# Modulation work moved to earlier FFNs, and four more FFN tiles by seven products, in a two-layer hybrid trunk

## The chip, the cores and the metric

The kernel runs on one core of a Trainium2 chip, in one launch. The metric is the device time of one execution in microseconds (us); 0.2% of it is 5.6 us.

## What is computed

Two layers of a trunk run over 640 tokens of width 1024: 128 of a prompt and 512 of a sample. Each layer has a SwiGLU FFN, a token mixing (state-space scan, long convolution, retention and attention side by side) and a second FFN. Shift, scale and gate of each of these three parts come from a product of the condition with a modulation matrix of 1024 x 9216 per layer.

```python
def trunk_layer(x, cond, lp, ssd_s0, ret_s0, ctx_kv):
    mod = (jax.nn.silu(cond) @ lp['w_mod'] + lp['b_mod'])[:, None, :]
    sh1, sc1, g1, sh2, sc2, g2, sh3, sc3, g3 = jnp.split(mod, N_MOD, axis=-1)
    nw = lp['norm_w']
    x = x + 0.5 * g1 * swiglu(modulate(rmsnorm(x, nw[0]), sh1, sc1), lp['ffn_w_in'][0], lp['ffn_w_out'][0])
    y, s_ssd, s_ret, k, v = token_mixing(modulate(rmsnorm(x, nw[1]), sh2, sc2), lp, ssd_s0, ret_s0, ctx_kv)
    x = x + g2 * y
    x = x + 0.5 * g3 * swiglu(modulate(rmsnorm(x, nw[2]), sh3, sc3), lp['ffn_w_in'][1], lp['ffn_w_out'][1])
```

`swiglu(h)` is `(silu(h @ w_gate) * (h @ w_up)) @ w_out` with an inner width of 2816, that is 22 tiles of 128.

## The kernel before

**Layout.** Activations are kept transposed: 8 tiles of 128 channels by 640 tokens, in two groups g of 320 columns. Every product of float32 values is made of three fp32r matmuls (`mm3`, L88: high by high, high by low, low by high). A weight tile is loaded as `raw` (512 KB), ScalarE casts it to `hi` (L76), and VectorE subtracts to get `lo` (`wsplit`, `tt`, L61); activations are split in the same way (`hh`, `hl`; in the FFN `gh`, `gl`). There are three buffers each of `raw`, `hi` and `lo`, and three PSUM buffers `mm`.

**The FFNs.** There are four: the first (layer 0, before the mixing) is `ffn`, all of its 22 inner tiles direct. The second (layer 0, after the mixing), the third (layer 1, before) and the fourth (layer 1, after) are `ffn7`. In `ffn7` the first `ndir` tiles are direct: a `direct` tile is a gate unit and an up unit for each group, 4 units of 24 matmuls, 96 in all. The other tiles are `quad` tiles: gate and up weights by the two token groups are taken as a product of 2 x 2 blocks, done with seven products instead of eight, 84 matmuls. For this VectorE makes sums of weights (`sa`, `sb`) and `sums(j)` makes sums of the normed tiles (`nv`) and splits them into factors (`th`, `tl`). `NDIR` gives the direct tiles of the second, third and fourth FFN: 2, 12, 2. The inner tiles come in chunks of 5, 5, 5, 4 and 3 (`FFN_CHUNKS`); after each of the first four, `down` multiplies the chunk by the output weights (8 tiles m by 2 groups) and VectorE accumulates into the residual `x` (L70).

**The modulations.** Apart from a few blocks at the start, which TensorE multiplies, VectorE makes all modulations (`modulation`, `modpiece`, L271): a step is a multiply-reduce of a 128x1024 weight tile `wm` against the silu of one of the two conditions (`condb`), output `wmj` being junk, with a row that reads the accumulator. A tile is two steps; a modulation (li, idx) is 8 tiles, 16 steps; `wm` has two buffers (`MBUF`). `todo` lists which modulations are made in which FFN. The FFN's code draws the steps: a rate is added to a credit after each half tile of a direct tile (`rates[0]`), after each m of a `down` (`rates[1]`) and after each quad (`rates[2]`), and a step is issued for each whole credit. What is left is issued before the last chunk.

```python
            def some(rate):
                credit[0] += rate
                while credit[0] >= 1.0:
                    next(mods, None)
                    credit[0] -= 1.0
```

**What sets the order.** The order on each engine is fixed at compile time: a list scheduler takes instructions by priority, largely the program's order, and fills in what is ready. `PIN` (`keep_in_program_order`) pins each modulation step to its place in the program. Each engine and each DMA queue (all loads are issued by SyncE) then runs its own instructions in that order.

Of the kernel before, what the change touches and what calls it, by code (L numbers as in the profile page):

```python
# [53 lines left out]
class Trunk:  # L54
# [486 lines left out]
    def ffn7(self, li, w, todo, ndir, rates, after_group):  # L541
        I, n = self.I, 2 * w
        pool = lambda name: self.tc.tile_pool(name=name, bufs=2, side="right", reuse_waits="tile")
        with pool("ws") as sp, pool("ffn") as mp, pool("mods") as modp, self.tmp():
            mods = self.modulation(todo, modp, bufs=MBUF, pin=PIN) if todo else iter(())
            self.G = []
            credit = [0.0]
# [8 lines that stand above are left out]
            def finish(q):  # L556
                for _ in q:
                    pass

            def down(ff, nk):  # L560

                G, self.G = self.G[:nk], self.G[nk:]
                for m in range(8):
                    hi, lo = self.wload(I["ffnoutA"][li, w, m, :, ff * 128 : (ff + nk) * 128], nk * 128)
                    for g in range(2):
                        ps = self.mmp.tile([128, 512], F32, tag="mm", name="mm")[:, :320]
                        self.mm3(ps, [(hi[:, k * 128 : (k + 1) * 128], lo[:, k * 128 : (k + 1) * 128]) + G[k][g]
                                      for k in range(nk)])
                        self.accumulate(li, n, m, g, ps)
                    some(rates[1])  # L570

            def direct(f):

                ws = [self.wload(I["ffnin"][li, w, 2 * f + i], 1024) for i in range(2)]
                sg = mp.tile([128, 640], F32, tag="sg", name="sg", bufs=2)
                gh = self.ring("gh", 640, F32R)
                gl = self.ring("gl", 640, F32R)
                for g in range(2):
                    c = slice(320 * g, 320 * g + 320)
                    self.act(sg[:, c], self.unit(ws[0], g, shifts=False), AF.Silu)  # L580
                    self.tt(sg[:, c], self.unit(ws[1], g, shifts=False), sg[:, c], MUL)
                    self.split(gh[:, c], gl[:, c], sg[:, c])
                    some(rates[0])
                self.G.append([(gh[:, 320 * g : 320 * g + 320], gl[:, 320 * g : 320 * g + 320]) for g in range(2)])

            ends = [sum(FFN_CHUNKS[: i + 1]) for i in range(len(FFN_CHUNKS))]
            for f in range(ndir):
                direct(f)
                if f < 2:
                    self.sums(f)  # L590
                if f + 1 in ends:
                    nk = FFN_CHUNKS[ends.index(f + 1)]
                    down(f + 1 - nk, nk)
            for j in range(2):
                self.split(self.hw[0][1][:, 2 * j : 2 * j + 2, 0:320], self.hw[1][1][:, 2 * j : 2 * j + 2, 0:320], self.V[0][j])
            prev = None
            for f in range(ndir, 22):
                q = self.quad(li, w, f, sp, mp, f == 21)
                next(q)
                if prev is not None:  # L600
                    next(prev)
                next(q)
                if prev is not None:
                    finish(prev)
                    if f in ends:
                        ci = ends.index(f)
                        down(f - FFN_CHUNKS[ci], FFN_CHUNKS[ci])
                prev = q
                some(rates[2])
            finish(prev)  # L610
            for _ in mods:
                pass
            nk = FFN_CHUNKS[-1]
            ws = [self.wload(I["ffnoutB"][li, w, b], 1024) for b in range(3)]
            G = self.G
            for g in range(2):
                for m in range(8):
                    if g and m == NPOS:
                        next(done, None)
                    ps = self.mmp.tile([128, 512], F32, tag="mm", name="mm")[:, :320]  # L620
                    parts = []
                    for k in range(nk):
                        b, j = divmod(m * nk + k, 8)
                        parts.append((ws[b][0][:, j * 128 : (j + 1) * 128],
                                      ws[b][1][:, j * 128 : (j + 1) * 128]) + G[k][g])
                    self.mm3(ps, parts)
                    self.accumulate(li, n, m, g, ps)
                    if li + 1 < NL or w == 0:
                        self.square(m, g)
                if g:  # L630
                    next(done, None)
                done = after_group(g)
                next(done, None)
            next(done, None)
# [777 lines left out]
    def run(self):  # L1412
        self.setup()
        with self.tc.tile_pool(name="start", bufs=2, side="right", reuse_waits="tile") as p, self.tmp():
            nc = self.nc
            cb = self.condb_start(p)
            self.xload(self.I["xT"])
            norms = [self.norm(0, 0, g, nc.vector, True) for g in range(2)]
            scale = self.modulation([(0, 1)], p, tiles=range(4, 8), bufs=SMB, cb=cb)
            shift = self.modulation([(0, 0)], p, tiles=range(2 * SPE, 8), bufs=SMB, cb=cb)  # L1420
            for j in range(2 + SPE):
                self.modulation_start(0, 1 if j < 2 else 0, p, range(j % 2, j % 2 + 1) if j < 4 else range(j - 2, j - 1))
                for gen in (scale, scale) if j < 2 else (shift,):
                    next(gen, None)
                for g in range(2):
                    if j == SORD[g] or j == SORD[2 + g]:
                        next(norms[g], None)
            for _ in shift:
                pass
            self.shifts(0, 0)  # L1430
            ahead = [self.wload(self.I["ffnin"][0, 0, i], 1024) for i in range(2)]
            for n in norms:
                next(n, None)
        kern = self.filters(range(NL))
        todo = [[(0, i) for i in range(2, 9)], [(1, 0), (1, 1)],
                [(1, i) for i in range(2, 8)], [(1, 8)]]
        for li in range(NL):
            def n1(g):
                if g == 0:
                    self.shifts(li, 1)  # L1440
                yield from self.norm(li, 1, g)
                self.xspill(li, g)

            def n2(g):
                yield from self.norm7(li, 2, g)

            def n3(g):
                if li + 1 < NL:
                    yield from self.norm7(li + 1, 0, g)
                else:  # L1450
                    self.store(g)
                    yield

            if li == 0:
                self.ffn(li, 0, todo[0], RATES[0], n1, ahead)
            else:
                self.ffn7(li, 0, todo[2], NDIR[1], RATES[2], n1)
                self.fac.close()
            for m in range(8):
                for g in range(2):  # L1460
                    self.tap(f"x1_{li}_{m}_{g}", self.x[m][g])
            self.mix(li, kern, n2)
            for m in range(8):
                for g in range(2):
                    self.tap(f"x2_{li}_{m}_{g}", self.x[m][g])
            self.ffn7(li, 1, todo[2 * li + 1], NDIR[2 * li], RATES[2 * li + 1], n3)
        self.fac.close()
# [7 lines left out]
RLAG = 1  # L1475
SLAG = 1
SB = 2
NDIR = 2, 12, 2
CB = 3
CGACT = True  # L1480
MBUF = 2
NPOS = 8
RATES = 2.0, (1.5, 1.0, 0.5), (2.2, 1.0, 1.0), (2.0, 1.0, 3.0)
PIN = True
WB = 3
EACT = 1
# [164 lines left out]
```

## Time and profile before

| | before |
|---|---|
| median of 3 runs | 2776.7 us (2774.94 to 2779.11) |
| the profiled execution | 2773.57 us |
| its span in the profile | 2771.8 us |
| granted TensorE clock, mean | 0.988 |
| TensorE busy | 96% |
| VectorE busy | 71% |
| ScalarE busy | 37% |

The span is what lies between the first and the last instruction of the profiled execution. Matmuls are pipelined: one is recorded as some 0.31 us while the next begins about 0.15 us after it, so that a count of matmul records in a stretch tells more than busy time. "mm" and "mb" are PSUM tiles, the second of a quad's first product.

### The profile page before, as it was taken

To read this page: it belongs to the slowest core of one execution; us is meant where nothing else is said; L and a number is where in the kernel's file an instruction comes from. 1 tells how busy PE (TensorE), PEld (TensorE's weight loads), DVE (VectorE), ACT (ScalarE), POOL (GpSimd) and SP (SyncE) were. 2 spreads that over 40 slices of the span, in tenths; PEclk is the share of its full clock that TensorE was granted. 3 is DMA by queue.
4 is the path that set the end of the run, shared out by engine and by line. 5 is a ranking of instruction groups with operands and counts; after the bars stand their busy time and mean duration, and the time that the engine had idled before them with its cause. 6 is when DMAs were issued, how large, how long until landed. Compare 5 with 4: busy or idle time off the path is not lost.

```text
span 2771.8 us, 45385 instructions
## 1 busy us (share of the span) xinstructions
PE 2671.7 (96%) x17870; PEld 2575.6 (93%) x17870; DVE 1959.7 (71%) x4050; ACT 1030.2 (37%) x2042; POOL 114.0 (4%) x191
## 2 busy tenths in 40 slices
PE   5999999999999989999999999998999998999999
PEld 3889999989999979999988999998999997999999
DVE  5886666665685687776667777787658578876666
ACT  3222222242455353433353223334335535343342
POOL 0000000020010020000020000002001002000000
PEclk9999999999999999999999999999999999999999
DMA  7435444431221323333213443334212132322222
GB/s 247 145 125 197 142 135 148 137 103 66 81 78 42 108 69 107 105 111 121 84 61 118 158 149 129 117 130 148 85 57 96 36 106 68 107 79 82 85 69 91
DMA packets 118389, 299.64 MB, mean 108 GB/s; under 512 B 19747, under 2 KB 42483, under 8 KB 117664
## 3 DMA queue, kind: packets, MB, share of 16 engines
q1 hardware_dynamic: 118176, 296.74, 32.6%
q8 instruction: 141, 2.31, 0.3%
q14 instruction: 72, 0.59, 0.1%
HBM read 282.49 MB, written 14.20 MB: 107 GB/s over the span
## 4 chain that ended last, share of the span: by engine, by line
PE 89%; DVE 5%; issue 2%; POOL 1%; ACT 1%; DMA 1%; SPq 0%; POOLq 0%; DVEq 0%; ACTq 0%
PE mm L88 68%; PE mx L88 10%; PE mc L88 6%; PE mb L88 3%; PE mx L93 2%; DVE lo L61 1%; POOL nsum L287 1%; DVE x L70 1%; DVE wmj L271 1%; ACT hi L76 0%; POOL nrs L120 0%; DVE hl L61 0%; DVE tl L61 0%; DVE nv L61 0%; DVE gl L61 0%
## 5 line engine op out<-in xcount | busy, mean ns | idle before, releaser
L88 PE MATMUL mm<-hh,lo 128*128 128x320 f32 (+2 forms) x2936 | 922.8, 315 | 13.0 <-DVE lo L61 13.0
L88 PE MATMUL mm<-hh,hi 128*128 128x320 f32 (+2 forms) x2936 | 927.6, 317 | 6.8 <-ACT hh L76 4.1
L88 PE MATMUL mm<-hl,hi 128*128 128x320 f32 (+2 forms) x2936 | 924.3, 315 | 2.5 <-DVE hl L61 2.1
L76 ACT CAST hi<-raw 128x1024 fp32r<-128x1024 f32 (+3 forms) x390 | 338.5, 868 | 779.0 <-PE mm L88 704.4
L88 PEld LDWEIGHTS mm<-hh,lo 128*128 128x128 f32 (+1 forms) x2936 | 558.8, 190 | 20.3 <-DVE lo L61 14.1
L88 PEld LDWEIGHTS mm<-hh,hi 128*128 128x128 f32 (+1 forms) x2936 | 557.1, 190 | 15.0 <-ACT hh L76 5.7
L88 PEld LDWEIGHTS mm<-hl,hi 128*128 128x128 f32 (+1 forms) x2936 | 556.9, 190 | 12.8 <-issue 5.1
L61 DVE TENSOR_TENSOR lo<-raw,hi 128x1024 fp32r<-128x1024 f32 (+3 forms) x390 | 387.6, 994 | 175.0 <-ACT hi L76 172.9
L88 PE MATMUL mm<-gh,hi 128*128 128x320 f32 x1408 | 438.4, 312 | 5.5 <-DVE x L70 5.5
L88 PE MATMUL mm<-gl,hi 128*128 128x320 f32 x1408 | 436.3, 311 | 0.5 <-DVE gl L61 0.3
L88 PE MATMUL mm<-gh,lo 128*128 128x320 f32 x1408 | 434.5, 309 | 0.0
L70 DVE SCALAR_TENSOR_TENSOR x<-mm,gate,x 128x128 f32<-128x128 f32 (+2 forms) x576 | 234.4, 434 | 175.2 <-PE mm L88 172.7
L271 DVE CUSTOM_DVE_ANT_0 wmj<-wm,condb 128x1024 bf16<-128x1024 f32 x264 | 321.2, 1217 | 3.0 <-ACT condb L73 1.2
L88 PEld LDWEIGHTS mm<-gh,hi 128*128 128x128 f32 x1408 | 265.1, 188 | 11.0 <-PE mm L88 9.0
L88 PEld LDWEIGHTS mm<-gl,hi 128*128 128x128 f32 x1408 | 265.3, 188 | 3.9 <-issue 1.8
L88 PEld LDWEIGHTS mm<-gh,lo 128*128 128x128 f32 x1408 | 265.0, 188 | 0.3 <-issue 0.2
L88 PE MATMUL mc<-th,lo 128*128 128x320 f32 x400 | 123.4, 309 | 0.0
L88 PE MATMUL mc<-th,hi 128*128 128x320 f32 x400 | 123.3, 308 | 0.0
L88 PE MATMUL mc<-tl,hi 128*128 128x320 f32 x400 | 123.3, 308 | 0.0
L287 POOL TENSOR_TENSOR nsum<-nsum,nsq 128x320 f32<-128x320 f32 x60 | 54.8, 914 | 1350.6 <-ACT nsq L73 945.8
L76 ACT CAST gh<-sg 128x640 fp32r<-128x640 f32 (+1 forms) x85 | 51.6, 607 | 103.7 <-DVE sg L61 103.7
L70 DVE SCALAR_TENSOR_TENSOR gu<-mm,cg,sg 128x128 f32<-128x128 f32 (+2 forms) x66 | 27.2, 435 | 76.2 <-ACT cg L76 49.0
(283 smaller groups left out, 3500.6 us busy)
## 6 DMA issues: line engine op xcount, KB each, us to landing
raw<-in_ffnin SPq DMA_DIRECT2D x176, 512.0 KB, 3.5
wm<-in_wmodT SPq DMA_DIRECT2D x132, 512.0 KB, 3.5
raw<-in_ffnoutA SPq DMA_DIRECT2D x96, 320.0 KB, 2.8
raw<-in_mixin SPq DMA_DIRECT2D x52, 512.0 KB, 3.4
raw<-in_ffnoutA SPq DMA_DIRECT2D x32, 256.0 KB, 2.6
wms<-in_wmod SPq DMA_DIRECT2D x12, 512.0 KB, 3.4
raw<-in_ffnoutB SPq DMA_DIRECT2D x12, 512.0 KB, 3.4
raw<-in_mixout SPq DMA_DIRECT2D x16, 384.0 KB, 2.9
```

The lines of the kernel that those rows point to most:

```text
L61: self.nc.vector.tensor_tensor(out, a, b, op=op)
L70: self.nc.vector.scalar_tensor_tensor(out, a, s, b, op0=op0, op1=op1)
L76: self.nc.scalar.copy(out, in_)
L88: return self.nc.tensor.matmul(out, lhsT=lhsT, rhs=rhs, start=start, stop=stop, **k)
L93: self.nc.tensor.transpose(out, in_, self.ident[b : b + n, b : b + n])
L271: return self.nc.vector.tensor_tensor_reduce(junk, raw, cb, 1.0, 0.0, op0=MUL, op1=ADD, accum_out=out)
L287: (adder or (self.nc.vector if g and m > 5 else self.nc.gpsimd)).tensor_tensor(s, s, sq, op=ADD)
```

## The change

Three things are edited. `todo` moves two modulations of layer 1 into the first FFN, so that (in steps) the four FFNs make 144, 32, 80 and 0 instead of 112, 32, 96 and 16. `RATES` follows: 2.7 instead of 2.0 per half tile in the first FFN after its first chunk, and in the second FFN none per direct half tile; in the third, none in tile 0 and 3.0 per half tile from then on (`rates = rates[1:]` at tile 1). `NDIR` makes 8 instead of 12 tiles of the third FFN direct, so 14 instead of 10 are quads. And `late` calls `sums(0)` and `sums(1)` of the third FFN after tiles 3 and 4 instead of tiles 0 and 1.

```diff
@@ ffn7 @@
             ends = [sum(FFN_CHUNKS[: i + 1]) for i in range(len(FFN_CHUNKS))]
+            late = 0 if ndir < 6 else 3
             for f in range(ndir):
+                if late and f == 1:
+                    rates = rates[1:]
                 direct(f)
-                if f < 2:
-                    self.sums(f)
+                if 0 <= f - late < 2:
+                    self.sums(f - late)
                 if f + 1 in ends:
@@ run @@
-        todo = [[(0, i) for i in range(2, 9)], [(1, 0), (1, 1)],
-                [(1, i) for i in range(2, 8)], [(1, 8)]]
+        todo = [[(0, i) for i in range(2, 9)] + [(1, 0), (1, 1)], [(1, 2), (1, 3)],
+                [(1, i) for i in range(4, 9)], []]
@@ constants @@
-NDIR = 2, 12, 2
+NDIR = 2, 8, 2
-RATES = 2.0, (1.5, 1.0, 0.5), (2.2, 1.0, 1.0), (2.0, 1.0, 3.0)
+RATES = 2.7, (0, 1.0, 0.5), (0, 3.0, 1.0, 1.0), (0, 0, 0)
```

TensorE's order goes from 16212 to 16163 rows, VectorE's from 3789 to 3813.

At the start of the second FFN, on VectorE, the order around the first quad's weights was the following, from the gated activations (`sg`) of the second tile to the first quad's `lo`:

```order
L61 TENSOR_TENSOR sg<-mm,sg 128x320
L61 TENSOR_TENSOR tl<-nv,th 128x2x320 x2
L61 TENSOR_TENSOR gl<-sg,gh 128x320
L271 ISA wmj,mod_108<-wm,condb 128x1024
L271 ISA mod_108 128x1
L61 TENSOR_TENSOR hl_106<-nv,hh_104 128x640
L271 ISA wmj,mod_108<-wm,condb 128x1024
L271 ISA mod_108 128x1
L61 TENSOR_TENSOR lo<-raw,hi 128x1024
```

Now the place reads as follows; the first `lo` is that of the second tile's up weights, the last that of the first quad:

```order
L61 TENSOR_TENSOR sg<-mm,sg 128x320
L61 TENSOR_TENSOR nv<-nv 128x640
L61 TENSOR_TENSOR tl<-nv,th 128x2x320
L61 TENSOR_TENSOR gl<-sg,gh 128x320
L61 TENSOR_TENSOR tl<-nv,th 128x2x320 x2
L61 TENSOR_TENSOR lo<-raw,hi 128x1024
L61 TENSOR_TENSOR nv<-nv 128x640
L61 TENSOR_TENSOR lo<-raw,hi 128x1024
```

The quad's `lo` has no modulation step ahead of it any more, and the second tile's up weights now stand behind the sums. The fourth FFN reads alike.

At the start of the third FFN, on VectorE, the order ahead of the second tile's gate weights (the last row) was:

```order
L61 TENSOR_TENSOR tl<-nv,th 128x2x320
L61 TENSOR_TENSOR gl<-sg,gh 128x320
L271 ISA wmj,mod_108<-wm,condb 128x1024
L271 ISA mod_108 128x1
L61 TENSOR_TENSOR nv<-nv 128x640
L271 ISA wmj,mod_108<-wm,condb 128x1024
L271 ISA mod_108 128x1
L61 TENSOR_TENSOR tl<-nv,th 128x2x320
L61 TENSOR_TENSOR mod_108<-mod_108,par_93 128x2
L61 TENSOR_TENSOR nv<-nv 128x640
L61 TENSOR_TENSOR lo<-raw,hi 128x1024
```

Now (the second `lo` is the gate's of the second tile, `hl` the low parts of the normed activations):

```order
L61 TENSOR_TENSOR hl_106<-nv,hh_104 128x640
L61 TENSOR_TENSOR sg<-mm,sg 128x320
L61 TENSOR_TENSOR lo<-raw,hi 128x1024
L61 TENSOR_TENSOR hl_106<-nv,hh_104 128x640 x2
L61 TENSOR_TENSOR gl<-sg,gh 128x320
L61 TENSOR_TENSOR nv<-nv 128x640 x3
L61 TENSOR_TENSOR lo<-raw,hi 128x1024
L61 TENSOR_TENSOR sg<-mm,sg 128x320
L61 TENSOR_TENSOR lo<-raw,hi 128x1024
```

The gate's `lo` moved up behind the gated activations of the first tile, and the modulation steps are gone from there; the sums (`nv`) are still in the first tiles.

In the last chunk of the first FFN, on VectorE, the first accumulations followed each other (`gu` is the gated product, `x_95` and `x_96` residual tiles):

```order
L61 TENSOR_TENSOR lo<-raw,hi 128x1024
L61 TENSOR_TENSOR gl<-gu,gh 128x320
L70 SCALAR_TENSOR_TENSOR x_95<-mm,gate_111,x_95 128x128
L70 SCALAR_TENSOR_TENSOR x_95<-mm,gate_111,x_95 128x192
L70 SCALAR_TENSOR_TENSOR x_96<-mm,gate_111,x_96 128x128
L70 SCALAR_TENSOR_TENSOR x_96<-mm,gate_111,x_96 128x192
```

Now three steps stand among them:

```order
L61 TENSOR_TENSOR gl<-gu,gh 128x320
L271 ISA wmj,mod_108<-wm,condb 128x1024
L271 ISA mod_108 128x1
L70 SCALAR_TENSOR_TENSOR x_95<-mm,gate_111,x_95 128x128
L61 TENSOR_TENSOR mod_108<-mod_108,par_93 128x2
L70 SCALAR_TENSOR_TENSOR x_95<-mm,gate_111,x_95 128x192
L70 SCALAR_TENSOR_TENSOR sc_110<-mod_108,par_93 128x2
L271 ISA wmj,mod_108<-wm,condb 128x1024
L271 ISA mod_108 128x1
L70 SCALAR_TENSOR_TENSOR x_96<-mm,gate_111,x_96 128x128
L271 ISA wmj,mod_108<-wm,condb 128x1024
L271 ISA mod_108 128x1
```

The last steps of the first FFN now stand at the front of its last chunk.

## Rows read from the trace of the kernel before

**Rows 1.** The page's first part: busy time, share, instructions of each engine.

```profile
PE 2671.7 (96%) x17870; PEld 2575.6 (93%) x17870; DVE 1959.7 (71%) x4050; ACT 1030.2 (37%) x2042; POOL 114.0 (4%) x191
```

**Rows 2.** Waits of TensorE over the whole span: total us, times, longest.

```profile
PE mb L88 <- DVE lo L61: 14.4, 2, 8.4
PE mm L88 <- DVE lo L61: 13.0, 6, 6.8
```

**Rows 3.** Windows by stretch; the first row names the columns.

```profile
core 0: us, PE busy (x) PEld busy (x) DVE busy (x) ACT busy (x) POOL busy (x), PEclk, DMA share, GB/s
210.00:569.00 359.00, 359.00 (x2432) 359.00 (x2432) 240.84 (x474) 95.15 (x182) 0.00 (x0) 1.00 0.44 148
1022.00:1036.00 14.00, 7.99 (x45) 7.72 (x44) 12.64 (x20) 4.70 (x8) 0.00 (x0) 0.76 0.29 93
1456.00:1484.00 28.00, 21.14 (x127) 20.63 (x127) 26.48 (x43) 11.85 (x20) 0.00 (x0) 0.88 0.27 94
1484.00:1680.00 196.00, 196.00 (x1328) 196.00 (x1328) 135.68 (x264) 43.95 (x70) 0.00 (x0) 1.00 0.47 151
1862.00:1890.00 28.00, 27.16 (x181) 26.48 (x180) 23.07 (x37) 14.40 (x23) 0.00 (x0) 1.00 0.43 142
2338.00:2366.00 28.00, 19.61 (x120) 19.36 (x119) 26.21 (x43) 10.58 (x18) 0.00 (x0) 0.82 0.33 104
2702.00:2744.00 42.00, 42.00 (x287) 41.98 (x286) 28.38 (x47) 16.56 (x25) 0.00 (x0) 1.00 0.26 89
```

**Rows 4.** TensorE's timeline: start, us, operation, idle before; three FFN starts.

```profile
1029.16 0.64 PE L88 MATMUL mb<-hh,lo 128*128 128x320 f32 x1 [6.01 <-DVE lo L61]
1029.59 0.47 PE L88 MATMUL mb<-hh,hi 128*128 128x320 f32 x1
1029.86 0.47 PE L88 MATMUL mb<-hl,hi 128*128 128x320 f32 x1
...
1471.05 0.64 PE L88 MATMUL mm<-hh,lo 128*128 128x320 f32 x1 [6.78 <-DVE lo L61]
...
2359.01 0.63 PE L88 MATMUL mb<-hh,lo 128*128 128x320 f32 x1 [8.39 <-DVE lo L61]
```

**Rows 5.** VectorE's timeline, start of the second FFN.

```profile
1008.61 1.22 DVE L61 TENSOR_TENSOR lo<-raw,hi 128x1024 fp32r<-128x1024 f32 x1
1009.75 0.48 DVE L61 TENSOR_TENSOR sg<-mm,sg 128x320 f32<-128x320 f32 x1
1010.15 0.81 DVE L61 TENSOR_TENSOR nv<-nv 128x640 f32<-128x640 f32 x1
1010.88 0.48 DVE L61 TENSOR_TENSOR gl<-sg,gh 128x320 fp32r<-128x320 f32 x1
1011.28 1.22 DVE L271 CUSTOM_DVE_ANT_0 wmj<-wm,condb 128x1024 bf16<-128x1024 f32 x1
1012.43 0.08 DVE L271 DVE_READ_ACCUMULATOR2_ANT mod<- 128x1 f32 x1
1012.43 0.82 DVE L61 TENSOR_TENSOR tl<-nv,th 128x640 fp32r<-128x640 f32 x1
1013.17 0.15 DVE L61 TENSOR_TENSOR mod<-mod,par 128x2 f32<-128x2 f32 x1
...
1027.89 1.22 DVE L61 TENSOR_TENSOR lo<-raw,hi 128x1024 fp32r<-128x1024 f32 x1
```

**Rows 6.** VectorE's timeline, start of the third FFN.

```profile
1469.78 1.22 DVE L61 TENSOR_TENSOR lo<-raw,hi 128x1024 fp32r<-128x1024 f32 x1
...
1486.91 0.49 DVE L61 TENSOR_TENSOR sg<-mm,sg 128x320 f32<-128x320 f32 x1 [1.48 <-PE mm L88]
...
1501.15 0.49 DVE L61 TENSOR_TENSOR sg<-mm,sg 128x320 f32<-128x320 f32 x1 [0.74 <-PE mm L88]
```

**Rows 7.** VectorE's timeline, last chunk of the first FFN.

```profile
572.02 0.68 DVE L70 SCALAR_TENSOR_TENSOR x<-mm,gate,x 128x128 f32<-128x128 f32 x2 [0.65 <-PE mm L88]
573.34 0.68 DVE L70 SCALAR_TENSOR_TENSOR x<-mm,gate,x 128x128 f32<-128x128 f32 x2 [0.65 <-PE mm L88]
```

**Rows 8.** The page's costliest groups and DMA issues: a modulation step and its load.

```profile
L271 DVE CUSTOM_DVE_ANT_0 wmj<-wm,condb 128x1024 bf16<-128x1024 f32 x264 | 321.2, 1217 | 3.0 <-ACT condb L73 1.2
...
wm<-in_wmodT SPq DMA_DIRECT2D x132, 512.0 KB, 3.5
```

## The prediction

> **What bounds the kernel now.** First the page's busy shares [rows 1]: TensorE is busy 96% of the span, VectorE 71%. So TensorE sets the time, and there are two ways to gain: fewer matmuls, or less of the roughly 100 us in which it stands. Then TensorE's waits by releaser [rows 2]: two waits on a `lo` ahead of a quad's first product sum to 14.4 us, six on a `lo` ahead of a direct unit to 13.0 us. The reader is to see that few places hold nearly all of it. TensorE's timeline gives three of them [rows 4]: 6.01 us at the start of the second FFN, 6.78 us at the third, 8.39 us at the fourth.
>
> The windows [rows 3] tell what these places cost altogether. At full clock TensorE records 1328 matmuls in 196 us, 6.776 a us, one every 0.148 us. Against that pace:
> - second FFN, 1022 to 1036: 45 records are worth 45/6.776 = 6.6 us, so 14 - 6.6 = 7.4 us are lost, with a granted clock of 0.76 in this stretch;
> - third FFN, 1456 to 1484: 127 records are 18.7 us, so 9.3 us lost, clock 0.88;
> - fourth FFN, 2338 to 2366: 120 records are 17.7 us, so 10.3 us lost, clock 0.82.
>
> The loss is the wait and then matmuls at half pace: behind the wait they follow each other every 0.27 us (1029.59 to 1029.86) [rows 4], against 0.148, which is the lower of the clock's two levels (1.2 GHz) against 2.4; TensorE had stood still before it fell. Loss less wait is 7.4 - 6.0 = 1.4, 9.3 - 6.8 = 2.5 and 10.3 - 8.4 = 1.9 us.
>
> Who is late there? VectorE is busy 12.64 of 14, 26.48 of 28 and 26.21 of 28 us in these windows [rows 3]. Its timeline [rows 5] shows an in-order queue in which modulation steps of 1.22 us stand with the sums (`nv`, `tl`) between the tile's own work and the `lo` that TensorE awaits, which begins at 1027.89 only. In the order of before, six steps stand there in the second FFN, four in the third, eight in the fourth. So these three stretches are VectorE's, though the kernel is TensorE's.
>
> **The change part by part.**
>
> *Four quads for four direct tiles.* A direct tile is 96 matmuls, a quad 84, so 48 fewer: 48/6.776 = **-7.1 us**. A direct tile's own duration agrees: 1501.15 - 1486.91 = 14.24 us [rows 6], 12/96 of it 1.78, four times 7.1. A quad's extra sums of weights lie on VectorE, which has room: 135.68 of 196 us in the direct stretch [rows 3]. The longest new wait would be at the switch from direct to quad, where `lo` of the weight sums stands close: between 0 and one `lo` of 1.22 us; I take **+0.5**.
>
> *Second FFN, no steps in the first two tiles.* Six steps of 1.2 us are 7.2 us, more than the wait of 6.0, so it goes: **-7.4** with its slow matmuls. What is late next: by the new order the `lo` of the second tile's up weights stands behind `sg`, `nv`, `tl`, `gl`, `tl`, `tl`. By the distances of their starts [rows 5] that is 0.40 + 0.73 + 0.74 + 0.40 + 0.74 + 0.74, and 1.14 for itself, 4.9 us after the tile's last unit; TensorE has one unit meanwhile (24 matmuls, 3.5 us). So a new wait of about **+1.5**. Whether the clock falls after so short a stop no row shows: between 0 and the 1.9 us that the three places lost on average; half, **+1.0**. Together -4.9; bounds -7.4 (no new wait) and 0 (the new waits are as long as the old).
>
> *Third FFN, no steps in tile 0.* The awaited `lo` of 1469.78 [rows 6] was the second tile's gate. In the new order it stands behind the first tile's work with no step ahead; -9.3, and I leave 0.5 for the sums still there: **-8.8**; bounds -9.3 and 0.
>
> *Fourth FFN, no steps at all.* Eight were ahead, 9.8 us against a wait of 8.4; the order is as in the second, so -10.3 + 1.5 + 1.0 = **-7.8**; bounds -10.3 and 0.
>
> *Third FFN's end.* Before, two steps are left over and issued ahead of the last chunk: 1862 to 1890 has 181 records, 26.7 of 28 us, 1.3 lost, while the fourth's end loses nothing (287 records in 42 us) [rows 3]. Now 88 credits are given for 80 steps: **-1.3**.
>
> *Where the steps go.* The first FFN gets 32 more. At 1.2 us these are 38 us on VectorE, which is busy 240.84 of 359 us there while TensorE is busy all 359 [rows 3]: (241 + 38)/359 = 78%. So they cost nothing as long as VectorE's room covers them. The cover is a unit of 3.5 us that hides up to three steps of 1.22 (3.7 us), since the next weights are split a unit or more ahead. The third FFN's later tiles go from 2.2 to 3.0 steps a half tile, 0.8 x 1.2 = 1 us more in 7.1: from 69% (135.68/196) to 83%. Steps bring loads too: 16 more of 512 KB in the first FFN, 3.5 us each [rows 8], ahead of weight loads in SyncE's queue; the DMA share there was 0.44 [rows 3], and the same loads leave the later FFNs. Nothing for both.
>
> *The first FFN's end.* Three steps now stand among the last chunk's first accumulations, 3.7 us on VectorE, while accumulations came 1.32 us apart [rows 7] and three PSUM buffers wait for them. Three buffers last about 4 us, so between 0 and 3.7: **+0.5**.
>
> *Later sums.* In the new order the `nv` rows of the third FFN are still in its first tiles, filled in by the scheduler. So this part does not do what it says, and costs nothing.
>
> Sum: -7.1 + 0.5 - 4.9 - 8.8 - 7.8 - 1.3 + 0.5 = **-28.9 us**. Against the profiled execution's 2773.6 that is 2744.7; the median of the runs is 3.1 us above that execution, so **2748 us** is the prediction for the median.
>
> **The rivals.**
>
> *Half of the starts' gain is given back.* The three starts yield 21.5 us by the sum. If the sums and the splits of activations, 0.7 us each and still there, keep VectorE full, about half goes into waits on other `lo`s with the clock falling behind each: 10.8 us back, 2759 us. For it speaks that VectorE was busy 90 to 95% of these windows [rows 3]; against it, that the steps removed are longer than the waits.
>
> *Only the matmuls count.* If TensorE's stops are simply replaced by equal ones, 2776.7 - 7.1 = 2770 us, just within faster. The Trainium skill, "Perfetto Trace Analysis", section "Identifying the Most-Contended Engine", says to optimise the engine of highest occupancy first, here TensorE at 96%, by which the rearranging of VectorE's work would yield little. The trace disagrees in the three windows, where VectorE comes last.
>
> *No new waits, or shorter ones than reckoned.* All lower bounds together: -7.1 - 7.4 - 9.3 - 10.3 - 1.3 = -35.4, 2741 us or a little less.
>
> *Slower: steps delay weights all along.* In the first FFN's 34 half tiles after the first chunk and the third's 14 after tile 0, up to three pinned steps, 3.7 us, stand ahead of a `lo`, a little more than a unit of 3.5. If each half tile lost 1 us, 48 us less 28.9 would be +19: 2796. It decides from 28.9/48 = 0.6 us a half tile. Against it: at 2.0 to 2.2 steps a half tile TensorE lost nothing in 359 and in 196 us [rows 3], and the share of VectorE stays at 83%.
>
> **How the numbers follow.** The forecast (2741 to 2756) gets 0.68, half given back (to 2764) 0.16, only the matmuls 0.08, no new waits (under 2741) 0.04, slower 0.04. Range 2738 to 2765: it takes in the first two, and 3 us under the lower bounds' 2741, for the runs themselves spread over 4; left out are the matmuls alone, slower, and a little below. 0.2%, 5.6 us, is about what a measurement can tell from no change: faster means under 2771.1. All cases but the last lie there, the matmuls alone half: 0.68 + 0.16 + 0.04 + 0.04 = 0.92; the other half is no change, 0.04; slower 0.04.
>
> **What would show it.** In the new profile: TensorE's waits on `lo` fall from 27 us to some 5; at the starts of the second and fourth FFN one wait of about 1.5 us ahead of an up unit, none ahead of the first quad; at the third no wait over 1 us; the first FFN without gaps at 78% of VectorE; no wait at the switch to quads over 1.2 us; VectorE's busy time nearly unchanged. The prediction is wrong if waits on `lo` or on `x` appear in each half tile of the first or third FFN, or if the second and fourth FFN keep waits of 4 us or more.

## The result, and the profile after

| | before | changed |
|---|---|---|
| median of the runs shown together | 2777.9 us (2774.94 to 2781.65, 4 runs) | 2745.74 us (2743.47 to 2748.28, 4 runs) |
| ratio | | 0.9884 (95% interval 0.9867 to 0.9901) |
| the profiled execution | 2773.57 us | 2743.99 us |
| its span | 2771.8 us | 2742.2 us |

The forecast was 2748 us for the median and 2744.7 for the profiled execution. The page's busy shares of the changed kernel answer to [rows 1]: 48 matmuls fewer, VectorE busy 20 us longer in a shorter span.

```profile
PE 2659.9 (97%) x17822; PEld 2563.3 (93%) x17822; DVE 1979.9 (72%) x4082; ACT 1038.5 (38%) x2057; POOL 114.7 (4%) x191
```

TensorE's waits by releaser in the changed kernel (total us, times, longest) answer to [rows 2]:

```profile
PE mm L88 <- DVE lo L61: 6.5, 6, 1.8
...
PE mm L88 <- DVE mod L61: 1.4, 1, 1.4
...
PE mm L88 <- DVE sc L70: 0.6, 1, 0.6
```

The waits ahead of a quad (`mb`, 14.4 us) are gone, and those of `mm` on a `lo` fell from 13.0 to 6.5 us. By TensorE's timeline only two of the six of [rows 2] stand ahead of a direct unit, both at the start of the third FFN: 6.78 us, which is gone, and 1.38 us, which stays; the other four, 1.78 and 0.66 us twice, stand in the two token mixings, which the change doesn't touch. New are two short ones on a step's small operations (`mod`, `sc`).

The windows of the changed kernel (columns as in [rows 3]) at the places of [rows 3]: the first FFN, the second's start in two pieces, the third's and the fourth's:

```profile
211.00:570.00 359.00, 359.00 (x2432) 358.99 (x2431) 275.73 (x552) 95.24 (x182) 0.00 (x0) 1.00 0.51 171
1010.00:1024.00 14.00, 14.00 (x95) 13.94 (x95) 13.81 (x21) 8.40 (x14) 0.00 (x0) 1.00 0.11 39
1024.00:1038.00 14.00, 14.00 (x97) 14.00 (x96) 12.97 (x19) 7.69 (x12) 0.00 (x0) 1.00 0.33 112
1456.00:1484.00 28.00, 28.00 (x191) 28.00 (x191) 27.97 (x45) 13.70 (x23) 0.00 (x0) 1.00 0.41 130
2310.00:2338.00 28.00, 28.00 (x188) 27.80 (x189) 26.79 (x40) 16.99 (x29) 0.00 (x0) 1.00 0.15 49
```

Where 45, 127 and 120 matmuls were recorded there are now 95 and 97 in 14 us, 191 and 188 in 28 us, all at clock 1.00: full pace, though VectorE is as busy as before. So its busy share alone does not make TensorE wait there; what stands ahead of the awaited `lo` does.

**Where the time came from.** Each norm begins with ten small matmuls (`mx<-ones,nsum`) per token group, and these cut both traces into the same stages. TensorE's timeline, before:

```profile
37.26 1.23 PE L88 MATMUL mx<-ones,nsum 128*64 128x1 f32 x10 [7.50 <-DVE nsum L287]
579.60 0.74 PE L88 MATMUL mx<-ones,nsum 128*64 128x1 f32 x10 [0.58 <-POOL nsum L287]
...
988.09 0.74 PE L88 MATMUL mx<-ones,nsum 128*64 128x1 f32 x10
1429.39 0.74 PE L88 MATMUL mx<-ones,nsum 128*64 128x1 f32 x10 [0.58 <-POOL nsum L287]
1443.21 0.74 PE L88 MATMUL mx<-ones,nsum 128*64 128x1 f32 x10 [0.57 <-DVE nsum L287]
1905.72 0.74 PE L88 MATMUL mx<-ones,nsum 128*64 128x1 f32 x10 [0.57 <-POOL nsum L287]
...
2315.61 0.74 PE L88 MATMUL mx<-ones,nsum 128*64 128x1 f32 x10
```

and changed:

```profile
37.54 1.23 PE L88 MATMUL mx<-ones,nsum 128*64 128x1 f32 x10 [7.50 <-DVE nsum L287]
583.03 0.74 PE L88 MATMUL mx<-ones,nsum 128*64 128x1 f32 x10 [0.58 <-POOL nsum L287]
...
991.39 0.74 PE L88 MATMUL mx<-ones,nsum 128*64 128x1 f32 x10
1425.36 0.74 PE L88 MATMUL mx<-ones,nsum 128*64 128x1 f32 x10 [0.58 <-POOL nsum L287]
1442.19 0.74 PE L88 MATMUL mx<-ones,nsum 128*64 128x1 f32 x10 [0.64 <-DVE nsum L287]
1886.50 0.74 PE L88 MATMUL mx<-ones,nsum 128*64 128x1 f32 x10 [0.58 <-POOL nsum L287]
...
2296.23 0.74 PE L88 MATMUL mx<-ones,nsum 128*64 128x1 f32 x10
```

The differences of these rows are the stages, in us. The experiments told of further on were cut in the same way, and those that do or undo one part stand in the last column:

| stage | before | changed | difference | other kernels |
|---|---|---|---|---|
| first FFN, from its second norm group to the next norm | 542.3 | 545.5 | +3.2 | |
| second FFN | 441.3 | 434.0 | -7.3 | before, without early steps 434.1; changed, with half of them 438.4 |
| norm between second and third FFN | 13.8 | 16.8 | +3.0 | 13.8 to 16.9 |
| third FFN | 462.5 | 444.3 | -18.2 | before, with later sums 452.8; changed, twelve direct 451.4 |
| fourth FFN to the end | 456.2 | 446.0 | -10.2 | changed, its steps back 457.4 |

These five sum to -29.5, and the profiled executions differ by 29.6. All other stages cancel: the norm behind the third FFN is 1.5 us shorter, the second mixing 1.9 longer, the others are within 0.5. Single executions of an FFN that no edit touches still differ by up to 1.5 us (the second FFN was 441.3 us in the kernel before and 442.8 in that kernel with later sums).

### The profile page after: what moved, and what is told of

Read it like the earlier page. It is cut to its first block, busy times and chain, and to the rows that moved or that the text cites. A ratio compares the mean times of both kernels' runs of the same rounds, so it can differ in the third digit from the quotient of the medians.

```text
span 2742.2 us, 45337 instructions
## 1 busy us (share of the span) xinstructions
PE 2659.9 (97%) x17822; PEld 2563.3 (93%) x17822; DVE 1979.9 (72%) x4082; ACT 1038.5 (38%) x2057; POOL 114.7 (4%) x191
## 4 chain that ended last, share of the span: by engine, by line
PE 90%; DVE 4%; POOL 2%; issue 1%; ACT 1%; DMA 1%; SPq 0%; POOLq 0%; DVEq 0%; ACTq 0%
PE mm L88 68%; PE mx L88 10%; PE mc L88 7%; PE mb L88 4%; PE mx L93 2%; DVE lo L61 1%; DVE x L70 1%; POOL nsum L287 1%; POOL nrs L120 1%; DMA E<-cumd 0%; DVE hl L61 0%; ACT hi L76 0%; DVE nsum L287 0%; DVE wmj L271 0%; DVE ndg L61 0%
## 5 line engine op out<-in xcount | busy, mean ns | idle before, releaser
L88 PE MATMUL mm<-hh,hi 128*128 128x320 f32 (+1 forms) x2856 | 901.1, 316 | 6.7 <-ACT hh L76 4.1
L88 PE MATMUL mm<-hh,lo 128*128 128x320 f32 (+1 forms) x2856 | 896.4, 315 | 6.5 <-DVE lo L61 6.5
L88 PE MATMUL mm<-hl,hi 128*128 128x320 f32 (+1 forms) x2856 | 898.1, 315 | 2.1 <-DVE hl L61 2.0
L88 PEld LDWEIGHTS mm<-hh,lo 128*128 128x128 f32 x2856 | 542.1, 190 | 14.0 <-DVE lo L61 7.5
L88 PEld LDWEIGHTS mm<-hh,hi 128*128 128x128 f32 x2856 | 540.5, 189 | 15.0 <-ACT hh L76 5.7
L88 PEld LDWEIGHTS mm<-hl,hi 128*128 128x128 f32 x2856 | 540.6, 189 | 12.0 <-issue 4.8
L88 PEld LDWEIGHTS mm<-gh,hi 128*128 128x128 f32 x1408 | 265.5, 189 | 12.6 <-PE mm L88 8.6
L88 PE MATMUL mc<-th,hi 128*128 128x320 f32 x432 | 133.2, 308 | 0.0
L88 PE MATMUL mc<-th,lo 128*128 128x320 f32 x432 | 133.2, 308 | 0.0
L88 PE MATMUL mc<-tl,hi 128*128 128x320 f32 x432 | 133.1, 308 | 0.0
L76 ACT CAST hi<-sb 128x1024 fp32r<-128x1024 f32 x54 | 56.6, 1049 | 68.2 <-PE mm L88 68.2
```

The source lines that it names most:

```text
L76: self.nc.scalar.copy(out, in_)
L88: return self.nc.tensor.matmul(out, lhsT=lhsT, rhs=rhs, start=start, stop=stop, **k)
```

## The experiments

Theory A: TensorE stood at these places for a `lo` that was late in VectorE's in-order queue, and what stands ahead of it there decides. Theory B: as in the prediction, the modulation steps alone matter and the later sums do nothing. Theory C: the steps' loads, ahead of the weights in SyncE's queue, made the waits. The kernel before ran beside each on the same chip, with medians of 2776.41 to 2777.9 us.

**Later sums alone.** The kernel before with only this:

```diff
-                if f < 2:
-                    self.sums(f)
+                if 0 <= f - (3 if ndir >= 6 else 0) < 2:
+                    self.sums(f - (3 if ndir >= 6 else 0))
```

> The kernel before with the later sums of the third FFN alone (modulation steps, their rates and the twelve direct tiles unchanged). Theory A, what stands ahead of a lo in VectorE's queue decides, whatever it is: in the new order the second tile's gate lo stands right behind the first tile's work, ahead of two of the four steps; the wait of 6.8 us at the start of the third FFN falls under 1 us, the stretch gains 7 to 9 us, the whole 2765 to 2767 us against 2774. Theory B, as the prediction had it, only the steps matter and the later sums do nothing: 2774 us within 3, and the wait stays near 6.8 us.

Measured: 2767.67 us beside 2776.41 of the kernel before; the third FFN 452.8 us, 9.7 less. TensorE's waits:

```profile
PE mb L88 <- DVE lo L61: 14.4, 2, 8.4
...
PE mm L88 <- DVE lo L61: 6.2, 5, 1.8
```

The wait of 6.8 us is gone, those of the second and fourth FFN (`mb`) stand untouched. VectorE's timeline there shows why, with the first tile's first `sg`, the `lo` behind it and the first step:

```profile
1461.46 0.49 DVE L61 TENSOR_TENSOR sg<-mm,sg 128x320 f32<-128x320 f32 x1
1461.87 1.22 DVE L61 TENSOR_TENSOR lo<-raw,hi 128x1024 fp32r<-128x1024 f32 x1
...
1464.87 1.22 DVE L271 CUSTOM_DVE_ANT_0 wmj<-wm,condb 128x1024 bf16<-128x1024 f32 x1
```

The first tile's two `lo` lie ahead of that `sg`, so this one is of the second tile's gate weights, the one that TensorE awaited. It begins 0.4 us behind the `sg`, ahead of all four steps and of all sums. In the kernel before, whose first `sg` stood here,

```profile
1457.15 0.48 DVE L61 TENSOR_TENSOR sg<-mm,sg 128x320 f32<-128x320 f32 x1
```

it began 12.6 us behind it, at 1469.78 [rows 6]. (In the new order printed for the third FFN under "The change" it is therefore the first `lo` that is the gate's, and the second is of the up weights.) So the later sums do bring the third FFN's gain, by themselves, with all the steps in place. Theory B has fallen.

**Early sums again.** The changed kernel with the sums of the third FFN called after tiles 0 and 1 again:

```diff
-            late = 0 if ndir < 6 else 3
+            late = 0
...
-                if late and f == 1:
+                if ndir >= 6 and f == 1:
```

> The changed kernel with the sums of the third FFN called after tiles 0 and 1 again (rates and all else as changed). Theory A: with no step in tile 0 the gate lo still stands ahead of the sums' second half, so a wait of 0 to 2 us appears there, the whole is 0 to 3 us slower than the changed kernel (2744 in its profiled execution). Theory B, later sums cost and bring nothing: no difference at all in the waits of that start. If the later sums carry the third FFN's gain alone, 7 to 9 us are lost again: 2751 to 2753 us.

Measured: the third FFN 445.0 us, 0.7 more than in the changed kernel (less than the 1.5 us by which the same FFN can differ), and no wait on a `lo` beyond those of the changed kernel (6.5 us, six times, here too). The whole was 2748.78 us, of which the stages that differ most are norms (the one after the first FFN 17.3 against 14.2 us), on which the edit has no hold. The gate's `lo` begins at 1460.20, 3.7 us behind the first `sg` of 1456.46. So the empty first tile carries the third FFN's start by itself, too: either of the two edits is enough, and the other then adds nothing that these runs can tell. (From 452.8 with the later sums to 451.4 with everything but the quads it is 1.4 us, about the 1.3 of the leftover steps at the stage's end.)

**No early steps in the second FFN alone**, on the kernel before:

```diff
-RATES = 2.0, (1.5, 1.0, 0.5), (2.2, 1.0, 1.0), (2.0, 1.0, 3.0)
+RATES = 2.0, (0, 1.0, 0.5), (2.2, 1.0, 1.0), (2.0, 1.0, 3.0)
```

> The kernel before with no modulation steps in the first two tiles of the second FFN (the steps left over are issued before its last chunk), all else as before. Theory A: the wait of 6.0 us on the first quad's lo goes with the matmuls at the lower clock behind it, 7.4 us less in the stretch; steps left over before the last chunk give back up to 1.3 us each for two or more; the whole 2766 to 2769 us. Rival, the sums alone keep VectorE full and the wait moves to another lo: 0 to 3 us gained.

Measured: 2769.69 us; the second FFN 434.1 us, 7.2 less, and of the two waits ahead of a quad one of 8.4 us is left, the fourth FFN's. The rival has fallen: the sums, left in place, do not make the wait.

**The loads without the steps.** The changed kernel with the fourth FFN's eight loads of modulation weights at their old places and rates; nothing reads them.

```diff
-            mods = self.modulation(todo, modp, bufs=MBUF, pin=PIN) if todo else iter(())
+            mods = self.modulation(todo, modp, bufs=MBUF, pin=PIN) if todo else self.loads(modp)
...
-RATES = 2.7, (0, 1.0, 0.5), (0, 3.0, 1.0, 1.0), (0, 0, 0)
+RATES = 2.7, (0, 1.0, 0.5), (0, 3.0, 1.0, 1.0), (2.0, 1.0, 3.0)
...
+    def loads(self, pool):
+        for mt in range(8):
+            raw = pool.tile([128, 1024], F32, tag="wm", name="wm", bufs=MBUF)
+            self.tc.keep_in_program_order(self.nc.sync.dma_start(out=raw, in_=self.I["wmodT"][1, 64 + mt]))
+            yield
+            yield
```

> The changed kernel with the eight loads of modulation weights put back in the fourth FFN at the places where it made them before, without the multiply-reduce steps on VectorE (loads that nobody reads). Theory A, the steps on VectorE made the wait of 8.4 us: no new wait on a lo, the whole within 2 us of the changed kernel. Rival C, the loads ahead of the weight loads in SyncE's queue made it: the wait on the first quad's lo comes back with 5 to 10 us.

Measured: 2743.10 us, the fourth FFN 446.2 us against 446.0, no wait ahead of a quad. So the transfers cost nothing that can be told. As nobody reads them, this run lacks one thing: in the kernel before, SyncE also stood, four times and 26.2 us in all between 2300 and 2362, until a step had freed a buffer of `wm`. ScalarE's timeline of the kernel before settles that; the casts that belong to the late `lo` of the second, third and fourth FFN are

```profile
1008.73 1.04 ACT L76 CAST hi<-raw 128x1024 fp32r<-128x1024 f32 x1
...
1461.47 1.06 ACT L76 CAST hi<-raw 128x1024 fp32r<-128x1024 f32 x1 [2.24 <-PE mm L88]
...
2336.24 1.04 ACT L76 CAST hi<-raw 128x1024 fp32r<-128x1024 f32 x1
```

Weights and `hi` of the awaited `lo` were there 18, 7 and 20 us before the `lo` began (1027.89, 1469.78, 2357.75). Theory C has fallen.

**The fourth FFN's steps back** in the changed kernel (and out of the third):

```diff
-                [(1, i) for i in range(4, 9)], []]
+                [(1, i) for i in range(4, 8)], [(1, 8)]]
...
-RATES = 2.7, (0, 1.0, 0.5), (0, 3.0, 1.0, 1.0), (0, 0, 0)
+RATES = 2.7, (0, 1.0, 0.5), (0, 3.0, 1.0, 1.0), (2.0, 1.0, 3.0)
```

> The changed kernel with the sixteen steps of the fourth FFN put back there at their old rates (and no longer made in the third). Theory A, the steps in VectorE's queue: the wait of about 8.4 us on the first quad's lo comes back with slow matmuls behind it, and the stretch from the fourth FFN's norm to the end takes 455 to 457 us against 446.0; the whole 2753 to 2755 us. If something else in the change (the loads, the clock) had brought that gain, 446 to 448 us stay.

Measured: 2756.16 us, the fourth FFN 457.4 us, and TensorE's timeline has the old row again:

```profile
2340.55 0.63 PE L88 MATMUL mb<-hh,lo 128*128 128x320 f32 x1 [8.37 <-DVE lo L61]
```

With the run above this settles the fourth FFN: the same loads without the multiply-reduces cost 0.2 us, with them 11.5 (455 to 457 us were expected; the wait is as expected).

**Half of the second FFN's early steps**, in the changed kernel:

```diff
-RATES = 2.7, (0, 1.0, 0.5), (0, 3.0, 1.0, 1.0), (0, 0, 0)
+RATES = 2.7, (0.75, 1.0, 0.5), (0, 3.0, 1.0, 1.0), (0, 0, 0)
```

> The changed kernel with half the steps (rate 0.75 instead of 0; 1.5 before) in the first two tiles of the second FFN. Theory A with TensorE's order counted: TensorE has a unit and ten more matmuls (5 us) ahead of the second tile's up unit, the lo stands 4.9 us behind, so the slack there is near nothing and one step more ahead of it makes a wait of about 1 us; the second FFN, 434.0 us between its norms in the changed kernel and 441.3 before, takes 435 to 437. Rival, a threshold at the quad's lo alone (three of six steps, 3.6 us, are within the slack): no wait, 434 us.

Measured: 2746.30 us, the second FFN 438.4 us, 4.4 more. Both expectations missed the place. TensorE's timeline:

```profile
1034.25 0.64 PE L88 MATMUL mc<-th,hi 128*128 128x320 f32 x1 [2.72 <-ACT hi L76]
1034.68 0.47 PE L88 MATMUL mc<-tl,hi 128*128 128x320 f32 x1
1034.95 0.47 PE L88 MATMUL mm<-th,hi 128*128 128x320 f32 x1
```

The wait is neither on the up weights nor on the first quad's `lo`, but on the high part of the quad's weight sums, and VectorE is late behind that, too: it makes those sums (`sa`) only after the steps.

```profile
1029.55 1.22 DVE L271 CUSTOM_DVE_ANT_0 wmj<-wm,condb 128x1024 bf16<-128x1024 f32 x1
...
1032.44 0.68 DVE L61 TENSOR_TENSOR sa<-sb,raw 128x512 f32<-128x512 f32 x1
```

ScalarE's cast of these sums, in the changed kernel and here:

```profile
1024.87 1.04 ACT L76 CAST hi<-sa 128x1024 fp32r<-128x1024 f32 x1
```

```profile
1033.15 1.04 ACT L76 CAST hi<-sa 128x1024 fp32r<-128x1024 f32 x1
```

Counted from the first tile's last `sg` (1011.74 there, 1013.79 here) it is done 14.2 and 20.4 us behind. Three steps of 1.2 us made it 6.2 us later, since other rows went ahead of `sa` with them. Of these, 3.5 us were covered, as in the changed kernel TensorE's first `mc` begins at 1029.38, 3.5 us behind the cast; 2.7 were waited for, and by the 0.27 us spacing behind the wait 1.7 us more went into matmuls at the lower clock level (1.2 GHz).

The up weights' `lo` had a step more ahead of it and was 6.1 us behind that `sg` instead of 5.0, but TensorE's order had changed with it: 18 instead of ten matmuls of the gate unit's other group stand ahead of the first that needs this `lo`. VectorE's row and two of TensorE's, the second of the pair at 1019.88 being that first one:

```profile
1018.69 1.22 DVE L61 TENSOR_TENSOR lo<-raw,hi 128x1024 fp32r<-128x1024 f32 x1
...
1019.88 0.49 PE L88 MATMUL mm<-hh,lo 128*128 128x320 f32 x2
1020.21 0.31 PE L88 MATMUL mm<-hh,hi 128*128 128x320 f32 x1
```

So the cover is no fixed number: the scheduler filled in what the later `lo` needed.

**Twelve direct tiles again** in the changed kernel:

```diff
-NDIR = 2, 8, 2
+NDIR = 2, 12, 2
```

> The changed kernel with twelve direct tiles in the third FFN again, all else as changed. Theory, four quads are worth only their 48 matmuls: the third FFN, from its own norm to the next one, takes 7 us more than in the changed kernel (444.3 us there), 451 to 452 us, with no wait at the switch to quads in either. Rival, the quads' extra work on VectorE gave part back: 3 to 5 us more only, with waits at the switch that go.

Measured: 2747.17 us, the third FFN 451.4 against 444.3 us: 7.1 more. Four quads are worth their 48 matmuls (7.1 us), as near as a stage can be read. The rival has fallen; in the changed kernel no wait stands at the switch to quads.

**Denser steps in the first FFN** of the changed kernel:

```diff
-RATES = 2.7, (0, 1.0, 0.5), (0, 3.0, 1.0, 1.0), (0, 0, 0)
+RATES = 3.0, (0, 1.0, 0.5), (0, 3.0, 1.0, 1.0), (0, 0, 0)
```

> The changed kernel with 3.0 instead of 2.7 steps per half tile in the first FFN, so that its steps are made before the last chunk. Theory: the two waits of 0.6 and 1.4 us at the first accumulations of the last chunk go with what follows them, the first FFN takes 543 us between its norms against 545.5, the whole 2 to 3 us less than the changed kernel. Rival, the denser steps push the weights' lo behind TensorE in the half tiles: 0.3 us or more per half tile, the first FFN 550 us or more and the whole slower than the changed kernel.

Measured: 2747.19 us (2745.14 to 2748.62), ratio 0.9892 (0.9876 to 0.9909), no better than the changed kernel, and the first FFN 545.4 against 545.5 us. Neither expectation held. The two waits of the changed kernel at the last chunk, TensorE's timeline,

```profile
572.24 0.38 PE L88 MATMUL mm<-gh,hi 128*128 128x320 f32 x1 [0.59 <-DVE sc L70]
...
575.18 0.38 PE L88 MATMUL mm<-gh,hi 128*128 128x320 f32 x1 [1.40 <-DVE mod L61]
```

are gone, but one of 1.1 us came in the fourth chunk's products (seen again in the last run below):

```profile
510.64 0.42 PE L88 MATMUL mm<-gh,lo 128*128 128x320 f32 x1 [1.12 <-DVE lo L61]
```

Counted from TensorE's last matmul of the first chunk's products (at some 226 us; up to there the rate is the same in all), the rest of the stage takes 353.7 us before, 355.5 at 3.0 and 356.2 at 2.7, so 1.8 and 2.5 us longer. The other 0.7 us of the changed kernel's +3.2 lies ahead, where single executions of the kernels differ by up to 2.3 us.

**A version meant to beat both.** The changed kernel with

```diff
-        todo = [[(0, i) for i in range(2, 9)] + [(1, 0), (1, 1)], [(1, 2), (1, 3)],
-                [(1, i) for i in range(4, 9)], []]
+        todo = [[(0, i) for i in range(2, 9)] + [(1, 0), (1, 1)], [(1, 2), (1, 3), (1, 4)],
+                [(1, i) for i in range(5, 9)], []]
...
-NDIR = 2, 8, 2
+NDIR = 2, 2, 2
-RATES = 2.7, (0, 1.0, 0.5), (0, 3.0, 1.0, 1.0), (0, 0, 0)
+RATES = 3.0, (0, 1.0, 1.0), (0, 1.0, 1.7), (0, 0, 0)
```

> A version meant to beat both: the changed kernel with 3.0 steps per half tile in the first FFN, 48 instead of 32 steps in the second (one per quad instead of a half), and in the third 64 steps (1.7 per quad) and only two direct tiles, 20 quads. Theory: six more quads for direct tiles are 72 matmuls or 10.6 us less, the first FFN's tail 2.5 us less, so 2730 to 2735 us, about 0.984 of the kernel before. Rival, VectorE, at 70% in quads without steps and two of 1.2 us more in 12.5, comes last in each quad: waits of 0.5 us or more in most quads of the third FFN, 2740 us or more.

Measured: 2735.87 us (2733.25 to 2741.14), ratio 0.9855 (0.984 to 0.987). The third FFN takes 436.6 us, 7.7 less than in the changed kernel, where 72 matmuls are worth 10.6; two waits on a `lo`, of 0.2 and 0.6 us, are new there, and what made the rest of the difference stays open. The rival, a wait in most quads, has fallen.

**The same with 2.8:**

```diff
-RATES = 3.0, (0, 1.0, 1.0), (0, 1.0, 1.7), (0, 0, 0)
+RATES = 2.8, (0, 1.0, 1.0), (0, 1.0, 1.7), (0, 0, 0)
```

> The version with two direct tiles and more steps in the second FFN, with 2.8 instead of 3.0 steps per half tile in the first FFN. Theory: at 2.8 all steps are still made before the last chunk, so no wait at its first accumulations; the wait of 1.1 us on a lo in the fourth chunk's down that came with 3.0 goes if the density made it, the first FFN takes 543 us or less between its norms, 1 us less than with 3.0; the whole 2733 to 2736 us. If that wait is the place's own, it stays at 1 us and the time is the same.

Measured: 2730.39 us (2730.22 to 2735.50), ratio 0.9832 (0.9815 to 0.9848), the fastest of all. The first FFN takes 543.2 us, 1.0 less than with 3.0, but not for the reason expected: all of it lies ahead of the end of the first chunk's products, from which both take 355.5 us, and the wait in the fourth chunk's products is there as before. The third FFN, without an edit between the two versions, takes 435.4 us and has no new wait on a `lo`.

```profile
508.16 0.41 PE L88 MATMUL mm<-gh,lo 128*128 128x320 f32 x1 [1.12 <-DVE lo L61]
```

So that wait does not hang on the density between 2.8 and 3.0. That 2.8 is faster than 3.0 is not shown: the intervals overlap, and the stages that differ most between the two are norms. That this version is faster than the changed kernel is: its interval ends at 0.9848, and the other's begins at 0.9867.

## Why the prediction was right

The measured 2745.74 us lies inside the range of 2738 to 2765, and the sum for the profiled execution, -28.9 us, stands against -29.6. It came out that near because misses cancelled: the second, third and fourth FFN gave 6.3 us more than forecast, and the first FFN and a norm took 5.7 us that were not.

- *Four quads, -7.1 and +0.5 at the switch.* The matmuls were worth 7.1 (the run with twelve direct tiles). The 0.5 did not come.
- *Second and fourth FFN, -4.9 and -7.8.* The mechanism was right: steps out of VectorE's queue ahead of the first quad, shown by the runs that do one and undo the other. The sizes were -7.3 and -10.2, the lower bounds of the two terms (-7.4 and -10.3). The step that failed is "TensorE has one unit meanwhile (24 matmuls, 3.5 us). So a new wait of about +1.5". In TensorE's order of the changed kernel, 24 matmuls of the gate unit, two of the up unit that need no `lo`, and ten of the gate unit's other group stand ahead of the first matmul that needs the up weights' `lo`: 36 x 0.148 = 5.3 us against 4.9. VectorE's timeline at this place is as reckoned:

```profile
1011.74 0.49 DVE L61 TENSOR_TENSOR sg<-mm,sg 128x320 f32<-128x320 f32 x1 [0.16 <-ACT sg L73]
...
1014.02 1.55 DVE L61 TENSOR_TENSOR tl<-nv,th 128x640 fp32r<-128x640 f32 x2
1015.49 1.22 DVE L61 TENSOR_TENSOR lo<-raw,hi 128x1024 fp32r<-128x1024 f32 x1
```

  The `lo` is done 1016.71 - 1011.74 = 5.0 us after `sg` began, and TensorE ran on, its first matmul with that `lo` beginning 0.1 us later:

```profile
1016.66 0.31 PE L88 MATMUL mm<-hh,hi 128*128 128x320 f32 x1
1016.81 0.37 PE L88 MATMUL mm<-hh,lo 128*128 128x320 f32 x1
```

  The order of VectorE was read, that of TensorE was assumed. That the ten matmuls saved the wait is argued from the order and these rows, and from the run with half of the early steps, where 18 stood there and a `lo` 1.1 us later met no wait either; a kernel without them was not tried.
- *Third FFN's start, -8.8 and its end, -1.3.* The stage gave -18.2, of which 7.1 are matmuls, so 11.1 against 10.1. But the step "this part does not do what it says, and costs nothing" was wrong. The `nv` rows were still in the first tiles, as read, but the second tile's gate `lo` had gone ahead of all of them, and the later sums alone brought 9.7 us in this stage. I had taken the next `lo`, of the up weights, for the gate's, and credited the modulation steps alone; either edit is enough, so a sum that adds up parts hid it.
- *The first FFN.* 32 more steps cost nothing in the half tiles: 2432 matmuls in 359 us before and now, with VectorE at 275.73/359 = 77% (78% forecast). The slower rival had no place to begin. The term "+0.5" for its end was mis-sized: two waits of 0.6 and 1.4 us, 2.5 us with what follows them.
- *What no step foresaw* is +3.0 in the norm between second and third FFN. The clock made it, and it is not the change's: two kernels that have the change's edits took 13.8 us there, as before, and the kernel before with one edit in the second FFN 16.9 (last section).

The rivals: new waits that give half back (2759 us) and the matmuls alone (2770) lie above the interval, which ends at 0.9901 x 2777.9 = 2750. The Trainium skill, "Perfetto Trace Analysis", section "Optimization Strategy", just behind the rule that I had weighed for the latter, says that the most-contended engine can change over a kernel's regimes. The traces agree: TensorE is at 96% over the span before, but from 1022 to 1036 it is busy 7.99 of 14 us and VectorE 12.64 [rows 3]. Of the 35.7 us that the three later FFNs gave, 7.1 are matmuls and 28.6 come from places where VectorE came last.

## What to carry to other kernels

Where an in-order engine feeds the bound one, look at what stands ahead of the awaited instruction at the few stage starts, not at busy shares: work of the same total, moved to where the queue has cover, gave here about four fifths of what the three later FFNs gained (28.6 of 35.7 us). Count the cover on the waiting engine from its own order, too, and in the kernel that will run: here the scheduler filled in ten matmuls, and 18 where the operand came later. And test each part of a change alone: two parts that each remove the same wait look like one that works and one that does nothing.

## What was not expected of the hardware

The same code took different times from run to run at the norms, by the granted clock. The stage between the norm groups of the second and third FFN was 13.8 us in three of the twelve profiled kernels, 15.4 in two and 16.8 or 16.9 in seven, and no edit lies in it. Two windows behind that norm's first matmuls (columns as in [rows 3]), of the changed kernel and then of the changed kernel with early sums:

```profile
1428.00:1435.00 7.00, 6.88 (x23) 6.02 (x24) 3.49 (x11) 3.63 (x8) 1.73 (x2) 0.52 0.00 0
```

```profile
1431.00:1438.00 7.00, 7.00 (x45) 6.56 (x46) 6.07 (x16) 6.30 (x16) 3.53 (x4) 1.00 0.00 0
```

The stop ahead of them, 0.8 us on `ndg`, was the same in both. The clock fell behind it in the first (0.52, near the lower level of 1.2 GHz) and not in the second (1.00, the level of 2.4), 23 matmuls against 45. Ahead of it both had run the same instructions. What decides it stays open. Differences of 3 us between single executions of such kernels can come from one norm, so parts are better compared stage by stage than by the whole.
